# SiLU and merge gates computed by tanh, and the work of a recurrence pair shifted in time: a change to a fused encoder-block kernel

## The chip, the cores and the metric

The kernel runs on one core of a Trainium2 chip. The metric is the device time of one execution in microseconds (us). Five engines work beside each other, each through its own instructions in order: PE (TensorE, matmuls, with PEld for its weight loads), DVE (VectorE, elementwise), ACT (ScalarE, elementwise functions and casts), POOL (GpSimd, used here only to issue DMAs) and SP (SyncE, which issues the other DMAs). An engine that waits for a result of another holds up all that is queued behind it.

## The reference

One encoder block over 256 tokens of width 2048, all in float32:

```python
xn = rms_norm(x, norm_pre_w)
u_lru, g_lru, q, k, v, g_attn, m_lru, m_attn = split(xn @ w_in)
u = centred_depthwise_conv(u_lru, conv_w, conv_b)          # width 4
h = rg_lru(u, ..., reverse=False) + rg_lru(u, ..., reverse=True)
y_a = h * silu(g_lru)
y_b = windowed_gqa(partial_rope(q), partial_rope(k), v, sink) * silu(g_attn)
merged = sigmoid(m_lru) * (y_a @ w_proj_a) + sigmoid(m_attn) * (y_b @ w_proj_b)
x = x + rms_norm(merged @ w_out, norm_post_w)

def rg_lru(u, ...):                                        # 16 blocks of 128 channels
    r, i = sigmoid(block_matmul(u, w_r) + b_r), sigmoid(block_matmul(u, w_i) + b_i)
    log_a = -8 * r * softplus(-lam)
    return scan(a=exp(log_a), b=sqrt(-expm1(2 * log_a)) * i * u)
```

## The kernel before

**Products.** A float32 product is made of three passes on reduced parts: high part of the weights by high part of the activations, high by low, and low by high. The parts of activations are made by `lag_parts`/`parts_of` (a cast on ACT to the high part, a subtraction on DVE to the low part, line 123). Part of the products are saved by a seven-product scheme (`add_seven`, L634 on), whose operands are differences of quarters of x; four of those differences (`e1` to `e4`) are stored away in DRAM and taken back three times by `sums_back` (L889), which splits them again in `parts`.

**Steps and half steps.** The weights stream from DRAM as tiles of 128 x 2048 floats, 1 MB each. One tile is one *step* of the list `steps`, made of two half steps of about 2.3 us of PE work each. The program is written half step by half step: `at(hs, fn)` puts `fn` at a half step, `soon(fn, d)` puts it `d` half steps after the present one, and the work due at a half step is issued ahead of that half step's matmuls. So the order on every engine is fixed by these numbers. The names wh, wl, raw and chain with a number are the high and low part and the loaded tile of the step with that number. At the first half of step i, SP issues the load of tile i+3 (`fetch`), ACT casts tile i+2 to its high part (`ahead`, L991), and one half step later DVE takes the low part (`low`, L983). Some tiles are not loaded anew but made by adding a second tile in place to one that has been used: `low` then has POOL issue an accumulating DMA onto the same buffer (L989); such a tile is called chain. raw, wh and wl each have three buffers.

**The recurrence.** Eight calls of `lru_pair(n, b)`, for n = 0, 2, ... 14, take two blocks each, twelve half steps apart. Within a pair the list at L525 gives each piece its half step, counted from b (one more is added to those above 5): the convolution (`centre` on ACT with its centre tap, `conv` on DVE with three taps of two blocks), the parts of u, the gates' matmuls (`gates(0)`, `gates(1)`, two PSUM banks each, out of four that `bank` gives) and their sigmoids, then Tanh, Exp, Square, `scale1`, Sqrt, the product with the gated input, the scans and `gate_out`. ACT computes its functions from tables, and the compiler puts an ACT_TABLE_LOAD where the next function isn't in the one that stands: by its order one table serves Sigmoid and Tanh, one Exp and Tanh, and one Sqrt.

**SiLU and merge gates.** `silu_evac` (L537) takes the product of a gate path out of PSUM (`total`, L224: one copy on ACT, one addition on DVE), applies Sigmoid two half steps later and multiplies on DVE one after that. `gate_take` (L553) applies Sigmoid to the merge products; their gates multiply the projections in `take_pa` and `take_pb`, and `ms_part` (L848) copies the merged sum into the tile that the last product reads. The attention heads (`head`, L756) run from about 475 us on: scores, a maximum on DVE (L773), exponentials on ACT (L780), the normalisation (L786, L788), and a transposition of the probabilities p on PE (pt, L794).

Of the kernel before, what the change touches and what calls it, by code (L numbers as in the profile page):

```python
# [14 lines left out]
F32 = mybir.dt.float32  # L15
# [5 lines left out]
P = 128  # L21
# [62 lines left out]
def body(ctx, tc, x, xT, wall, wlru, pvec, npost, ident_d, mask_d, rope_d, out):  # L84
# [63 lines left out]
    def soon(fn, d=1):  # L148
        at(now[0] + d, fn)
# [216 lines left out]
    at(ROWS, row_scale)  # L366


    rtok = const.tile([P, 2], F32, name="rtok")

    def token_scale():
        for t in range(2):
            dg = small.tile([P, P], F32, tag="diag", name=f"diag{t}", bufs=1)
            nc.vector.tensor_tensor(dg, rbc[:, t * P:(t + 1) * P], ident, ALU.mult)
            nc.scalar.activation(dg, dg, AF.Copy, accum_out=rtok[:, t:t + 1])

    at(ROWS + 3, token_scale)

# [66 lines left out]
    def lru_pair(n, b):  # L445
# [71 lines left out]
        def gate_out():  # L517
            h = v["gr"]
            y = sgl[n // 4][:, n % 4:n % 4 + 2]
            nc.vector.tensor_tensor(h[:, 0:2], h[:, 0:2], h[:, 2:4], ALU.add)  # L520
            nc.vector.tensor_tensor(y, h[:, 0:2], y, ALU.mult)
            v.clear()

        at(max(b - 1, 7), load)
        for d, fn in (  # L525
            (-1, lambda: [centre(j) for j in range(2)]), (0, lambda: conv(0)), (1, lambda: conv(1)), (2, weights), (3, u_parts),
            (6, lambda: gates(0)), (7, lambda: gates(1)), (7, lambda: sigmoids(0)), (8, lambda: sigmoids(1)),
            (9, lambda: decays("th", AF.Tanh, cpos, 0)), (9, lambda: decays("th", AF.Tanh, cpos, 1)), (9, gated),
            (10, lambda: decays("a", AF.Exp, cneg, 0)), (11, lambda: decays("a", AF.Exp, cneg, 1)),
            (11, lambda: nc.scalar.activation(v["gr"], v["a"], AF.Square)), (12, scale1),  # L530
            (13, lambda: nc.scalar.activation(v["th"], v["th"], AF.Sqrt)),
            (16, lambda: nc.vector.tensor_tensor(v["gi"], v["gi"], v["th"], ALU.mult)),
            (17, scans), (19, gate_out),
        ):
            at(b + d + (G if d > 5 else 0), fn)

    def silu_evac(units_list, n, late=False):  # L537
        def done(ps):
            if n % 4 == 0:
                units_list.append(unit(f"sg{n}"))  # L540
            dst = units_list[n // 4][:, n % 4:n % 4 + 2]
            sg = unit(f"sig{n}", F32, (P, 2, S)) if late else half_unit(f"sig{n}", "p")
            total(dst, ps)
            soon(lambda: nc.scalar.activation(sg, dst, AF.Sigmoid), 2)
            soon(lambda: nc.vector.tensor_tensor(dst, dst, sg, ALU.mult), 3)
        return done

    def u_evac(n):
# [1 line left out]

    tm, sm, ms, whole = {}, {}, {}, {}

    def gate_take(units_of, c, t, ps, scale=1.0):  # L553
        if c not in units_of:
            units_of[c] = unit(f"mg{c}", F32, (P, 2, 512))
        nc.scalar.activation(units_of[c][:, t], ps, AF.Sigmoid, scale=scale)
        if units_of is sm and c < 2:
            return
        name = "sm" if units_of is sm else "tm"
        written[name, c] = written.get((name, c), 0) + 1  # L560
        if written[name, c] == 2:
            soon(lambda: gone.update({(name, c): put_away(f"{name}{c}", units_of.pop(c))}), AWAY)
# [1 line left out]
    gone, written = {}, {}  # L564

    def gate_evac(units_of, c, scaled=False):
        return lambda t, ps: gate_take(units_of, c, t, ps, rtok[:, t:t + 1] if scaled else 1.0)

    kv = {}

# [185 lines left out]
    def head(hd, qh, ql, b):  # L756
# [49 lines left out]

        def gate_out():
            y = sga[g][:, j]
            nc.vector.tensor_tensor(y, v["o"][:, 0], y, ALU.mult)
            v.clear()  # L810

        for d, fn in ((0, scores), (1, expo), (2, powers), (3, normalise), (5, flip), (6, p_parts), (9, values), (10, gate_out)):
# [12 lines left out]

    def take_pa(c, t, d):
        g = tm[c][:, t]
        nc.vector.tensor_tensor(g, d, g, ALU.mult)

    def take_pb(c, t, d):  # L830
        g = sm[c][:, t]
        nc.vector.tensor_tensor(g, d, g, ALU.mult)
        nc.vector.tensor_tensor(g, tm[c][:, t], g, ALU.add)
        if t == 1:
            held = {}
            soon(lambda: ms_flip(c, held), 3)
            for q in range(2):
                soon(lambda q=q: ms_part(c, q, held), 4 + q)
# [9 lines left out]
    def ms_part(c, q, held):  # L848
        a = pair_unit(f"ms{2 * c + q}")
        ms[2 * c + q] = a  # L850
        if q == 0:
            whole[c] = unit(f"mw{c}")
        w = whole[c][:, 2 * q:2 * q + 2]
        nc.scalar.copy(w, held.pop(q))
        lag_parts(a[:, :, 0], a[:, :, 1], w)

    def branch(name, m, y, take):
# [31 lines left out]
    def sums_back(r):  # L889
        def back(d, n):  # L890
            l = take_back(f"e{r}{d}", kept[d], F32R, (P, 8, P))

            def parts():
                h = unit(f"e{r}{d}h", F32R, (P, 8, P))
                lag_parts(h, l, l.bitcast(F32))
                again[r][d] = (h, l)

            at(n - 7, parts)

        for d, n in (("e1", 4), ("e4", 6), ("e3", 8), ("e2", 10)):  # L900
            n = 2 * steps.index(woven[14 * (r + 1) + n])
            at(n - 16, lambda d=d, n=n: back(d, n))
# [192 lines left out]
```

## Time and profile before

| | |
|---|---|
| runs shown | 887.29, 888.70, 888.81 us; median 888.7 |
| profiled execution | 889.92 us, its span 888.1 us |
| granted TensorE clock, mean | 0.997 |
| busy: PE, PEld | 871.8 us, 746.2 us |
| busy: DVE, ACT, POOL | 717.8 us, 648.5 us, 44.1 us |
| DMA | 230.89 MB, mean 260 GB/s |

The span is the time from the first to the last instruction in the trace; the time of the execution has some more around it. Busy times are sums over the instructions of an engine, and PE's matmuls are pipelined, so that a busy PE says only that it had a matmul under way. A row of the trace's timeline gives start and duration in us, engine, line of the kernel, operation, output<-input with shapes and types, the count, and in brackets the idle time ahead of it with the releaser: the engine and line whose result came last. The row of a group of instructions gives the line, engine, operation, operands and count, then busy us in all and the mean in ns, then the idle time ahead of it. In a row of the waits the three numbers are the total in us, how many times, and the longest.

### The profile page before, as it was taken

The page shows a single profiled execution, that of the slowest core. Times are in us where ns is not written, and L with a number is a line of the kernel's source. Part 1 is how long each engine was busy: PE and PEld are TensorE (multiplying, and loading weights), DVE is VectorE, ACT ScalarE, POOL GpSimd, SP SyncE. Part 2 cuts the span into 40 slices and gives each one's busy share as a digit, 9 for nine tenths or more (in the row PEclk, how much of TensorE's full clock was granted, in tenths as well). Part 3 has the DMA queues.
Part 4 walks back from the last instruction along what each step waited for, and adds up shares of the span by engine and source line. Part 5 has one row for each costly group of instructions (what it writes and reads, how often), then busy time and mean ns, then how long its engine had stood idle before and what let it go on. Part 6 is the DMA issues. An engine that isn't in the chain of part 4 may idle for free.

```text
span 888.1 us, 11537 instructions
## 1 busy us (share of the span) xinstructions
PE 871.8 (98%) x4494; PEld 746.2 (84%) x4494; DVE 717.8 (81%) x763; ACT 648.5 (73%) x762; POOL 44.1 (5%) x57
## 2 busy tenths in 40 slices
PE   8999999999999999999999999999999999999996
PEld 8888888888888888888877788888888888888885
DVE  5987897978969699897967878778897767757886
ACT  6978579787796977879688877967966454547653
POOL 0000000010000100000000000000000000100000
PEclk9999999999999999999999999999999999999998
DMA  8746977997998988888877976897966996998894
GB/s 323 273 169 243 324 212 265 279 308 204 315 339 301 238 229 291 234 341 245 248 208 280 245 270 214 203 278 275 260 249 237 271 246 194 320 287 317 227 275 161
DMA packets 38935, 230.89 MB, mean 260 GB/s; under 512 B 4320, under 2 KB 5216, under 8 KB 15456
## 3 DMA queue, kind: packets, MB, share of 16 engines
q1 hardware_dynamic: 31248, 179.19, 53.6%
q0 software_dynamic: 7200, 50.33, 29.4%
q8 instruction: 35, 0.57, 0.2%
q10 hardware_dynamic: 432, 0.63, 0.2%
q14 instruction: 20, 0.16, 0.0%
HBM read 220.70 MB, written 9.44 MB: 259 GB/s over the span
## 4 chain that ended last, share of the span: by engine, by line
PE 77%; ACT 9%; DVE 6%; DMA 5%; issue 2%; DVEq 0%; SPq 0%; ACTq 0%
PE ga L209 5%; PE gl L209 5%; ACT wh L995 3%; PE u L209 3%; DVE wl L985 3%; DMA chain<-wall_dram 3%; PE gl L211 3%; PE ga L211 3%; PE pa__5505 L240 2%; PE q__4370 L240 2%; PE q__4968 L240 2%; PE ml__622 L240 2%; PE ml L240 2%; PE pa__5865 L240 2%; PE o__6883 L240 2%; PE o L240 2%
## 5 line engine op out<-in xcount | busy, mean ns | idle before, releaser
L985 DVE TENSOR_TENSOR wl<-raw,wh 128x2048 fp32r<-128x2048 f32 x112 | 256.0, 2288 | 60.3 <-ACT wh L995 60.3
L995 ACT CAST wh<-raw 128x2048 fp32r<-128x2048 f32 x112 | 214.0, 1912 | 56.5 <-DMA raw<-wall_dram 20.8
L985 DVE TENSOR_TENSOR wl<-chain,wh 128x2048 fp32r<-128x2048 f32 x68 | 155.4, 2287 | 37.9 <-ACT wh L995 37.9
L995 ACT CAST wh<-chain 128x2048 fp32r<-128x2048 f32 x68 | 129.9, 1912 | 59.6 <-DMA chain<-wall_dram 23.5
L989 POOL DMA_DIRECT2D chain<-wall_dram x46 | 40.2, 874 | 768.6 <-DVE wl L985 761.0
L209 PE MATMUL ga<-xn,wh 128*128 128x512 f32 x256 | 62.9, 391 | 0.0
L209 PE MATMUL gl<-xn,wh 128*128 128x512 f32 x256 | 62.2, 390 | 0.0
L209 PEld LDWEIGHTS gl<-xn,wh 128*128 128x128 f32 x256 | 47.6, 188 | 9.3
L209 PEld LDWEIGHTS ga<-xn,wh 128*128 128x128 f32 x256 | 47.4, 188 | 9.1
L209 PE MATMUL u<-xn,wh 128*128 128x512 f32 x192 | 46.8, 391 | 0.0
L209 PEld LDWEIGHTS u<-xn,wh 128*128 128x128 f32 x192 | 35.6, 188 | 7.1 <-ACT wh L995 0.3
L211 PEld LDWEIGHTS ga<-xn,wl 128*128 128x128 f32 x256 | 32.8, 191 | 1.3
L211 PEld LDWEIGHTS gl<-xn,wl 128*128 128x128 f32 x256 | 32.8, 191 | 1.2
L211 PE MATMUL gl<-xn,wl 128*128 128x256 f32 x256 | 33.2, 283 | 0.0
L211 PE MATMUL ga<-xn,wl 128*128 128x256 f32 x256 | 33.2, 283 | 0.0
L211 PEld LDWEIGHTS u<-xn,wl 128*128 128x128 f32 x192 | 24.6, 191 | 0.9
L211 PE MATMUL u<-xn,wl 128*128 128x256 f32 x192 | 24.9, 283 | 0.0
L470 DVE SCALAR_TENSOR_TENSOR up<-up,pv 128x255 f32<-128x255 f32 (+1 forms) x48 | 22.8, 482 | 1.1
L122 ACT CAST ph<-pt 128x512 fp32r<-128x512 f32 x16 | 9.4, 585 | 17.2 <-PE pt L794 13.2
L509 DVE SCALAR_TENSOR_TENSOR th<-gr,th 128x1024 f32<-128x1024 f32 x8 | 9.8, 1225 | 13.6 <-ACT gr L530 13.6
L399 PE MATMUL u_ps<-xs,wh 128*128 128x256 f32 x128 | 18.6, 288 | 1.8 <-ACT wh L115 1.8
L190 PE MATMUL gate<-uh,lwh 128*128 128x256 f32 x64 | 18.2, 285 | 2.1 <-ACT gi L494 2.1
(568 smaller groups left out, 1978.8 us busy)
## 6 DMA issues: line engine op xcount, KB each, us to landing
raw<-wall_dram SPq DMA_DIRECT2D x115, 1024.0 KB, 7.0
chain<-wall_dram POOLq DMA_DIRECT2D x46, 1024.0 KB, 9.6
chain<-wall_dram SPq DMA_DIRECT2D x22, 1024.0 KB, 4.9
lraw<-wlru_dram SPq DMA_DIRECT2D x8, 512.0 KB, 7.1
raw<-wall_dram SPq DMA_DIRECT2D x4, 512.0 KB, 8.0
tm_away<-mg SPq DMA_DIRECT2D x4, 512.0 KB, 9.4
xee_away<-xee SPq DMA_DIRECT2D x4, 512.0 KB, 8.3
ya_away<-sg SPq DMA_DIRECT2D x4, 512.0 KB, 10.3
```

What stands on the lines that cost most here:

```text
L122: nc.scalar.copy(h, src)
L190: nc.tensor.matmul(ps, wh, xh, start=start, stop=False)
L209: nc.tensor.matmul(ps, wh[:, sl], a, start=k == 0, stop=k == KT - 1)
L211: nc.tensor.matmul(ps[:, 1], wl[:, sl], a[:, 0], start=False, stop=False)
L240: nc.tensor.matmul(got[t], a[:, m], w[:, j * 512:(j + 1) * 512], start=k == 0 and m == 0 and not low, stop=low and k == KT - 1)
L399: nc.tensor.matmul(ups[b // 2][:, b % 2, 0], w[:, sl], a[:, m], start=k == 0 and n == 0, stop=k == KT - 1 and n == 2)
L470: nc.vector.scalar_tensor_tensor(u[:, a:b], up[:, a + tap - 2:b + tap - 2], cw[:, tap:tap + 1], u[:, a:b], ALU.mult, ALU.add)
L509: nc.vector.scalar_tensor_tensor(v["th"], v["gr"], 1.0, v["th"], ALU.add, ALU.mult)
L985: nc.vector.tensor_tensor(lows[i][:, sl], t, highs[i][:, sl].bitcast(F32), ALU.subtract)
L989: nc.gpsimd.dma_start(raws[n], wall[rows_of[steps[n][0]]], accum_op=ALU.add)
L995: nc.scalar.copy(highs[i][:, sl], t)
```

## The change

In place of sigmoid(z) stands (1 + tanh(z/2)) / 2. SiLU's Sigmoid and the merge gates' become Tanh with a scale of 0.5; the addition of 1 goes into the following DVE multiplication, which becomes a SCALAR_TENSOR_TENSOR; and the factor one half goes into the recurrence's and the heads' `gate_out` and into the copy of `ms_part`. The recurrence's own gates stay Sigmoid. In a pair, the convolution is put twelve half steps ahead (the centre tap nineteen), the second gates and all from the second sigmoids to Sqrt one half step later, and behind Sqrt comes a one-column activation `warm` that brings the next Sigmoid table (Tanh for the last pair). The splits of x's differences in `sums_back` are put three half steps sooner.

```diff
         for t in range(2):
...
-            nc.scalar.activation(dg, dg, AF.Copy, accum_out=rtok[:, t:t + 1])
+            nc.scalar.activation(dg, dg, AF.Copy, scale=0.5, accum_out=rhalf[:, t:t + 1])
...
-            nc.vector.tensor_tensor(y, h[:, 0:2], y, ALU.mult)
+            nc.vector.scalar_tensor_tensor(y, h[:, 0:2], 0.5, y, ALU.mult, ALU.mult)
...
-            (-1, lambda: [centre(j) for j in range(2)]), (0, lambda: conv(0)), (1, lambda: conv(1)), (2, weights), (3, u_parts),
-            (6, lambda: gates(0)), (7, lambda: gates(1)), (7, lambda: sigmoids(0)), (8, lambda: sigmoids(1)),
-            (9, lambda: decays("th", AF.Tanh, cpos, 0)), (9, lambda: decays("th", AF.Tanh, cpos, 1)), (9, gated),
-            (10, lambda: decays("a", AF.Exp, cneg, 0)), (11, lambda: decays("a", AF.Exp, cneg, 1)),
-            (11, lambda: nc.scalar.activation(v["gr"], v["a"], AF.Square)), (12, scale1),
-            (13, lambda: nc.scalar.activation(v["th"], v["th"], AF.Sqrt)),
+            ((-20, lambda: [centre(j) for j in range(2)]) if n else (-1, lambda: [centre(j) for j in range(2)])), (-12 if n else 0, lambda: conv(0)), (-11 if n else 1, lambda: conv(1)), (2, weights), (3, u_parts),
+            (6, lambda: gates(0)), (7, lambda: sigmoids(0)), (8, lambda: gates(1)), (9, lambda: sigmoids(1)),
+            (10, lambda: decays("th", AF.Tanh, cpos, 0)), (10, lambda: decays("th", AF.Tanh, cpos, 1)), (10, gated),
+            (11, lambda: decays("a", AF.Exp, cneg, 0)), (12, lambda: decays("a", AF.Exp, cneg, 1)),
+            (12, lambda: nc.scalar.activation(v["gr"], v["a"], AF.Square)), (13, scale1),
+            (14, lambda: nc.scalar.activation(v["th"], v["th"], AF.Sqrt)),
+            (14, lambda: nc.scalar.activation(warm, eps, AF.Sigmoid if n < 14 else AF.Tanh)),
             (16, lambda: nc.vector.tensor_tensor(v["gi"], v["gi"], v["th"], ALU.mult)),
             (17, scans), (19, gate_out),
...
-            soon(lambda: nc.scalar.activation(sg, dst, AF.Sigmoid), 2)
-            soon(lambda: nc.vector.tensor_tensor(dst, dst, sg, ALU.mult), 3)
+            soon(lambda: nc.scalar.activation(sg, dst, AF.Tanh, scale=0.5), 2)
+            soon(lambda: nc.vector.scalar_tensor_tensor(dst, sg, 1.0, dst, ALU.add, ALU.mult), 3)
...
-        nc.scalar.activation(units_of[c][:, t], ps, AF.Sigmoid, scale=scale)
+        nc.scalar.activation(units_of[c][:, t], ps, AF.Tanh, scale=scale)
...
-            nc.vector.tensor_tensor(y, v["o"][:, 0], y, ALU.mult)
+            nc.vector.scalar_tensor_tensor(y, v["o"][:, 0], 0.5, y, ALU.mult, ALU.mult)
...
-        nc.vector.tensor_tensor(g, d, g, ALU.mult)
+        nc.vector.scalar_tensor_tensor(g, g, 1.0, d, ALU.add, ALU.mult)
...
-        nc.scalar.copy(w, held.pop(q))
+        nc.scalar.activation(w, held.pop(q), AF.Copy, scale=0.5)
...
-            at(n - 7, parts)
+            at(n - 10, parts)
```

The built programs have 41 table loads before and 29 now on ACT, and eight one-column activations more. PE, SP and POOL have as many instructions as before, SP and POOL in the same order.

The first place is PE at the gates of pair 14, near 450 us. A name such as gate14_11 is the PSUM bank of the pair's gates (second block, second direction), mbn7_ is the accumulator of a seven-product step, and wh95 its weights. Before:

```order
L650 MATMUL mbn7_3818<-wl94_3866,e1e2h_3829 128x512 x4
L190 MATMUL gate14_10_3970<-uh14_3880,lwh14_3861 128x256
...
L192 MATMUL gate14_11_3977<-uh14_3880,lwl14_3862 128x256
L650 MATMUL mbn7_3818<-wh95_3901,e1e2h_3829 128x512
L650 MATMUL mbn7_3818<-wh95_3901,e1e2_3700 128x512
...
L604 MATMUL q0p_4003<-ident_97,q0t_3932 128x128 x8
```

And of the change:

```order
L651 MATMUL mbn7_3836<-wl94_3873,e1e2h_3799 128x512 x4
L651 MATMUL mbn7_3836<-wh95_3908,e1e2h_3799 128x512
L651 MATMUL mbn7_3836<-wh95_3908,e1e2_3716 128x512
...
L190 MATMUL gate14_10_3992<-uh14_3887,lwh14_3868 128x256
...
L192 MATMUL gate14_11_3999<-uh14_3887,lwl14_3869 128x256
L605 MATMUL q0p_4006<-ident_97,q0t_3939 128x128 x8
```

The matmuls of step 95's first half now stand ahead of the pair's second gates.

The second place is ACT behind the gates of the same pair, from about 460 to 477 us. th14, a14 and gr14 are the pair's decays and gates, q0p a rotated query, mg3 a merge gate, wh98 to wh101 the casts of the weights. Before:

```order
L505 ACT_TABLE_LOAD
...
L556 ACT_TABLE_LOAD
...
L505 ACT_TABLE_LOAD
L505 ACTIVATE a14_4048<-gr14_3984,cneg_163 128x256 x2
L530 ACTIVATE gr14_3984<-a14_4048 128x1024
L995 CAST wh99_4075<-chain87_3603 128x2048
L531 ACT_TABLE_LOAD
L531 ACTIVATE th14_4019<-th14_4019 128x1024
L995 CAST wh100_4107<-raw100_4069 128x2048
L995 CAST wh101_4133<-raw101_4104 128x2048
```

And of the change:

```order
L557 ACTIVATE mg3_4057<-mbt0_3311 128x512
L505 ACT_TABLE_LOAD
L505 ACTIVATE a14_4075<-gr14_3977,cneg_163 128x256 x2
L996 CAST wh99_4079<-chain87_3607 128x2048
L505 ACTIVATE a14_4075<-gr14_3977,cneg_163 128x256 x2
L530 ACTIVATE gr14_3977<-a14_4075 128x1024
L996 CAST wh100_4113<-raw100_4073 128x2048
L531 ACT_TABLE_LOAD
L531 ACTIVATE th14_4048<-th14_4048 128x1024
L532 ACT_TABLE_LOAD
L532 ACTIVATE warm_77<-eps_78 128x1
L996 CAST wh101_4141<-raw101_4110 128x2048
```

Sqrt with its table load stood ahead of wh100's cast and now stands behind it, followed by a further table load and `warm`. The three table loads for the first Exp of the decays (L505), for the merge gates (L556) and for the second Exp are one load now: the merge gates, as a Tanh at L557, stand ahead of it and need none.

The third place is ACT in pair 6, near 255 us, where the copy of `total` (the SiLU's product out of PSUM) is followed by the weight casts. Before:

```order
L226 COPY total_2330<-ga6_2243 128x512
L995 CAST wh52_2332<-raw52_2282 128x2048
L122 CAST e0e1h_2341<-e0e1_2148 128x1024
L544 ACT_TABLE_LOAD
L544 ACTIVATE sig6_2329<-sg4_1877 128x512
L995 CAST wh53_2353<-raw53_2324 128x2048
```

And of the change:

```order
L226 COPY total_2343<-ga6_2241 128x512
L996 CAST wh52_2345<-raw52_2284 128x2048
L531 ACT_TABLE_LOAD
L531 ACTIVATE th6_2254<-th6_2254 128x1024
L532 ACT_TABLE_LOAD
L532 ACTIVATE warm_77<-eps_78 128x1
L545 ACTIVATE sig6_2342<-sg4_1886 128x512
L996 CAST wh53_2365<-raw53_2337 128x2048
```

Sqrt, ahead of `total` before, now stands behind it, with two table loads where there was one. On DVE of the same pair, before:

```order
L521 TENSOR_TENSOR sg4_1702<-gr6_2201,sg4_1702 128x512
L985 TENSOR_TENSOR wl55_2419<-chain47_2055,wh55_2418 128x2048
L227 TENSOR_TENSOR up10_2458<-u10_2380,total_2459 128x512
L985 TENSOR_TENSOR wl56_2462<-raw56_2414,wh56_2461 128x2048
L470 SCALAR_TENSOR_TENSOR up8_2006<-up8_2006,pv_95 128x254
L470 SCALAR_TENSOR_TENSOR up8_2006<-up8_2006,pv_95 128x255 x2
L123 TENSOR_TENSOR e0e4_2327<-e0e4_2327,e0e4h_2475 128x1024
```

And of the change:

```order
L521 SCALAR_TENSOR_TENSOR sg4_1706<-gr6_2192,sg4_1706 128x512
L123 TENSOR_TENSOR e0e4_2340<-e0e4_2340,e0e4h_2430 128x1024
L986 TENSOR_TENSOR wl55_2433<-chain47_2058,wh55_2432 128x2048
L227 TENSOR_TENSOR up10_2473<-u10_2392,total_2474 128x512
L986 TENSOR_TENSOR wl56_2477<-raw56_2426,wh56_2476 128x2048
```

The low part of the stored difference e0e4 now stands ahead of the low part of step 55's weights, and the convolution of the next pair (L470) no longer stands behind them.

More of the change, by code (lines that the diff above doesn't have):

```diff
@@ L366, in body @@
     at(ROWS, row_scale)
-    rtok = const.tile([P, 2], F32, name="rtok")
+    rhalf = const.tile([P, 2], F32, name="rhalf")
     def token_scale():
@@ L551, in body, with gate_take @@
     tm, sm, ms, whole = {}, {}, {}, {}
-    def gate_take(units_of, c, t, ps, scale=1.0):
+    def gate_take(units_of, c, t, ps, scale=0.5):
         if c not in units_of:
             units_of[c] = unit(f"mg{c}", F32, (P, 2, 512))
-        nc.scalar.activation(units_of[c][:, t], ps, AF.Sigmoid, scale=scale)
+        nc.scalar.activation(units_of[c][:, t], ps, AF.Tanh, scale=scale)
         if units_of is sm and c < 2:
@@ L566, in gate_evac @@
     def gate_evac(units_of, c, scaled=False):
-        return lambda t, ps: gate_take(units_of, c, t, ps, rtok[:, t:t + 1] if scaled else 1.0)
+        return lambda t, ps: gate_take(units_of, c, t, ps, rhalf[:, t:t + 1] if scaled else 0.5)
     kv = {}
@@ L827, in take_pa @@
         g = tm[c][:, t]
-        nc.vector.tensor_tensor(g, d, g, ALU.mult)
+        nc.vector.scalar_tensor_tensor(g, g, 1.0, d, ALU.add, ALU.mult)
     def take_pb(c, t, d):
         g = sm[c][:, t]
-        nc.vector.tensor_tensor(g, d, g, ALU.mult)
+        nc.vector.scalar_tensor_tensor(g, g, 1.0, d, ALU.add, ALU.mult)
         nc.vector.tensor_tensor(g, tm[c][:, t], g, ALU.add)
```

## The prediction

> **What bounds the kernel now.** First the engine totals, then the stretches of 50 us, then what the weight loads of TensorE waited for, since PE runs its instructions in order and each such wait stops it.
>
> ```profile
> span 888.1 us, 11537 instructions
> PE 871.8 (98%) x4494; PEld 746.2 (84%) x4494; DVE 717.8 (81%) x763; ACT 648.5 (73%) x762; POOL 44.1 (5%) x57
> ```
> ```profile
> 400.00:450.00 50.00, 50.00 (x242) 42.24 (x242) 39.36 (x36) 37.39 (x39) 4.38 (x5) 1.00 0.90 254
> 450.00:500.00 50.00, 45.06 (x222) 36.95 (x222) 40.47 (x55) 45.72 (x63) 2.60 (x3) 1.00 0.78 222
> ```
> ```profile
> PEld pt L794 <- ACT p L788: 3.5, 4, 1.7
> PEld gate L190 <- ACT gi L494: 2.5, 2, 2.0
> PEld mlq L650 <- DVE wl L985: 1.1, 1, 1.1
> PEld q__4035 L240 <- ACT wh L995: 1.0, 1, 1.0
> PEld gate L191 <- DVE ul L123: 0.3, 1, 0.3
> PEld u L209 <- ACT wh L995: 0.3, 1, 0.3
> ```
>
> PE is busy 98% of the span, and the change keeps every matmul, so only PE's stops can be won. The columns of the stretches are length, then busy time (and instructions) of PE, PEld, DVE, ACT and POOL, the granted clock and DMA. Between 450 and 500 us PE loses 5 us and ACT is the fullest engine, 45.7 of 50; in the stretch before, nothing is lost. The six rows of waits (total, times, longest) are PE's stops after the start: 3.5+2.5+1.1+1.0+0.3+0.3 = 8.7 us. That is the ceiling. No table load, cast or convolution counts unless one of these stops hangs on it, or a new one arises.
>
> **What costs the same.** Tanh takes the place of Sigmoid on the same shapes, and a SCALAR_TENSOR_TENSOR that of a TENSOR_TENSOR:
>
> ```profile
> L509 DVE SCALAR_TENSOR_TENSOR th<-gr,th 128x1024 f32<-128x1024 f32 x8 | 9.8, 1225 | 13.6 <-ACT gr L530 13.6
> L532 DVE TENSOR_TENSOR gi<-gi,th 128x1024 f32<-128x1024 f32 x8 | 9.7, 1217 | 0.0
> L545 DVE TENSOR_TENSOR sg<-sg,sig 128x512 f32<-128x512 f32 x16 | 10.9, 684 | 0.0
> L556 ACT ACT_TABLE_LOAD x6 | 7.7, 1283 | 0.1
> L780 ACT ACT_TABLE_LOAD x6 | 7.7, 1283 | 0.1
> ```
>
> 1225 against 1217 ns on the same shape: the 56 exchanged VectorE instructions cost nothing (bounds: below, nothing can be won on them; above, the rule under the rivals). The half-scaled copies of ms_part stay one pass over 512 columns. Twelve table loads fall away (41 to 29): those of L556 and L780 that alternated while heads ran, 12 x 1.283 = 15.4 us of ACT. Most of it lies beside PE's work, so I count it only at the stops. Per pair of the recurrence the three loads stay (Exp, Sqrt, and one moved from the SiLU to right behind Sqrt), plus a one-column activation that I take at 0.3 us from the 128x2 row below (bounds 0 and 0.5, the shortest 128x256 ACTIVATE).
>
> **The stop at 453 us (second gates one half step behind).**
>
> ```profile
> 447.74 1.90 ACT L995 CAST wh<-chain 128x2048 fp32r<-128x2048 f32 x1 [7.74 <-DMA chain<-wall_dram]
> 449.55 1.07 ACT L578 COPY q0t<-q__3753 128x512 f32<-128x512 f32 x2
> 450.50 1.91 ACT L995 CAST wh<-raw 128x2048 fp32r<-128x2048 f32 x1
> 452.67 0.48 ACT L494 ACTIVATE gi<-gate,pv 128x256 f32<-128x256 f32 x1
> ```
> ```profile
> 433.28 0.86 POOL L989 DMA_DIRECT2D chain<-wall_dram  x1 [2.66 <-DVE wl L985]
> ```
> ```profile
> 453.21 0.19 PEld L190 LDWEIGHTS gate<-uh,lwh 128*128 128x128 f32 x1 [2.01 <-ACT gi L494]
> 454.03 0.19 PEld L650 LDWEIGHTS mbn<-wh,e1e 128*128 128x128 f32 x1
> 454.26 0.19 PEld L650 LDWEIGHTS mbn<-wh,e1e2h 128*128 128x128 f32 x1
> ```
>
> Pair 14's fourth gate bank is only free when ACT has read the first, and ACT is late because it stood 7.74 us before a cast (step 95) whose chained weights landed at 447.7. In the new order six matmuls of mbn7 (0.23 us each by the last two rows, 1.4 us) go ahead of the second gates. The release itself, 453.2, stays tied to the landing. That transfer is issued at 433.3, when wl91 is done. By the additions below wl91 comes at most 1.7 us later (a cast 1.0, a difference's split of 512 columns 0.7), but the queue still holds the transfer of the step ahead, whose wl comes earlier in the pair; I take 0.5 us for the landing (bounds 0 and 1.7; nearer to 0, as 14.4 us pass from issue to landing, most of it behind others). So PE leaves the gates having gained **1.4 - 0.5 = 0.9 us** over the old run (bounds -0.3 and 1.4 plus what is won before). This covers everything ahead of it: the 0.5 us stop of pair 10 (same cause, landing not involved) and the 0.3 of ul10 and of u go away, but PE only arrives sooner at the same landing.
>
> **What the moved work does to the weights of each pair.** In each pair the Sqrt, its table load, the next table load and the one-column activation now stand between `total` and the weight cast, and lag parts of x's differences are split three half steps sooner.
>
> ```profile
> 219.50 2.28 DVE L985 TENSOR_TENSOR wl<-chain,wh 128x2048 fp32r<-128x2048 f32 x1
> 271.28 2.28 DVE L985 TENSOR_TENSOR wl<-chain,wh 128x2048 fp32r<-128x2048 f32 x1
> 277.71 1.22 DVE L123 TENSOR_TENSOR e0e<-e0e,e0e4h 128x1024 fp32r<-128x1024 f32 x1
> 224.50 2.95 DVE L470 SCALAR_TENSOR_TENSOR up<-up,pv 128x254 f32<-128x254 f32 x6
> ```
> ```profile
> 222.39 0.87 PEld L650 LDWEIGHTS mlq<-wl,xn 128*128 128x128 f32 x4
> 275.03 0.87 PEld L650 LDWEIGHTS kvq<-wl,e0e1h 128*128 128x128 f32 x4
> 203.16 0.57 ACT L226 COPY total<-ga 128x512 f32<-128x512 f32 x1
> 205.55 1.28 ACT L544 ACT_TABLE_LOAD   x1
> ```
>
> Low parts of pair 4 end at 221.78, loaded at 222.39: 0.6 us in hand; pair 6 has 275.03 - 273.56 = 1.5. Sqrt and its load take 1.28 + 1.06 = 2.34 us (the rows of 205.55 here and of 472.60 below). ACT may start `total` that much sooner, but hardly more than 1.7 us, as PE's result must be there; it pays 2.34 + 0.3 after it: the cast, and VectorE's row behind it, come 1.0 us later. Pair 4: 0.35 us of new wait. Pair 6: 1.0 + 1.22 (e0e4's low parts now ahead of wl55) - 1.5 = 0.7. Pairs 10 and 12 I put below pair 4, at 0.1 and 0.2. Pair 2 (mlq's 1.1 us in the list of waits) 0.2 more; pair 8, without a difference there, none. Sum 1.55 us; bounds 0 (ACT idle enough) and 1.9 each, a whole cast. They fall before the landing, where PE waits anyway: PE would arrive at the last gate with some 0.4 us left to wait, so they cost nothing up to there, and one for one beyond 2.0 us. The convolution's 2.95 us and the two centres per pair move twelve and twenty half steps ahead into VectorE's and ACT's idle time (the releaser is ACT's casts there), at nothing; if that cover were gone they would add to the same weights, at most 2.95 a pair. What was taken away behind `u` only widens margins. SP's and POOL's queues keep their order; only the moment of a chained issue moves with wl.
>
> **The stops at 475, 486 and 496 us.**
>
> ```profile
> 469.39 1.89 ACT L995 CAST wh<-chain 128x2048 fp32r<-128x2048 f32 x1
> 472.60 1.06 ACT L531 ACTIVATE th<-th 128x1024 f32<-128x1024 f32 x1
> 473.56 3.69 ACT L995 CAST wh<-raw 128x2048 fp32r<-128x2048 f32 x2
> 480.96 0.28 ACT L781 ACTIVATE es<-nm,pv 128x2 f32<-128x2 f32 x1
> 485.42 0.91 ACT L788 ACTIVATE p<-p,rd 128x256 f32<-128x256 f32 x2 [2.38 <-DVE rd L786]
> ```
> ```profile
> 482.05 0.69 DVE L514 TENSOR_TENSOR_SCAN gr<-a,gi 128x256 f32<-128x256 f32 x1
> 485.16 0.17 DVE L786 RECIPROCAL rd<-dn 128x2 f32<-128x2 f32 x1
> ```
> ```profile
> 485.98 0.14 PEld L794 LDWEIGHTS pt<-ident,p 128*128 128x128 f32 x1 [1.68 <-ACT p L788]
> 496.36 0.14 PEld L794 LDWEIGHTS pt<-ident,p 128*128 128x128 f32 x1 [1.33 <-ACT p L788]
> ```
>
> I walk ACT's queue from 453.2 + 0.5. At 475 PE waited for wh100, cast from 473.56. Ahead of it now two loads are gone (2.6 us) and Sqrt with its load (2.34 us) stands behind it: about 4.9 less 0.5, so ready near 471; PE comes at 473.5. That stop goes: **1.0 us**. Then come load, Sqrt, load, one column (3.9 us) and wh101, which ends at 477.1 as before. VectorE then runs wl101 (2.3) and what it ran from 482.05 to 485.33, four scans, a difference and the reciprocal (3.3): 482.7. PE's row came 0.65 us behind the reciprocal's end, so 483.35; PE, 0.9 + 1.0 us sooner, is there at 484.30 - 1.9 = 482.4 and still waits some 1.0, where it waited 1.68: **0.6 us**. From there p1: between p0's scaling at 485.42 and PE's row at 496.36 lie 10.9 us, of them two loads (L556, L780) that fall away, 2.6. Set off at 482.8 that gives 491.1 to 492, as q1t and a cast may wait for their inputs; PE comes at 495.03 - 2.5 = 492.5. That stop goes: **1.6 us**, its 1.33 and some 0.25 in which the array drains (taken from the start-to-start gaps of PE's rows there). Later heads have no stop now, and less ACT work.
>
> Sum: 0.9 + 1.0 + 0.6 + 1.6 = **4.1 us**. The profiled execution is the span of 888.1 and some 1.8 us around it, 889.9; less 4.1 that is 885.8. The runs shown have a median of 888.7, which I put the change on: **884.6 us**.
>
> **Rivals.** (a) *Everything goes*: all stops but mlq's vanish and no pair waits; 8.7 - 1.1 = 7.6, less the 0.2 us that the array still drains in each: 882. For it: the landing may come sooner, as wl93 is done sooner. Against: VectorE's order at 483.
> (b) *The chained transfer becomes the bound*: step 95's weights, in flight from 433.3 to 447.7 beside two ordinary weight tiles, fall behind them by one tile's 4.1 us (1 MB at the 254 GB/s of the stretch from 400 to 450); the walk shifts whole, 4.1 - 4.1 = 0: 888.7. For it: wl91 comes later; against: the queue's earlier transfer hardly moves.
> (c) *Slower*: the weight casts of pairs 2, 4, 6, 10 and 12 slip by a further whole cast (1.9 us) each, since Sqrt's operand, VectorE's scale1, is itself late in the compressed chain. Price 5 x 1.9 = 9.5, the first 1.0 free: 893. It turns the sign once the pairs' waits grow by 5.1 us. Against: ACT's square ends before `total` may start in each pair that I walked.
> (d) *The exchanged instruction is slow*: at 1.37 us instead of 0.68 for silu's product and the recurrence's gate, 1.4 us more ahead of those same five weights, 7 - 1.0 = 6: 890.6. The two rows of 1225 and 1217 ns speak against it. The Trainium skill, "Vector Engine (DVE) Microarchitecture Reference", "7. Points that are easy to get wrong", states such a halved rate for this instruction with two non-bf16 SBUF sources; by that rule this rival holds, and this trace disagrees.
> (e) *It doesn't do what it says*, the loads staying: excluded, as the built order has 29.
>
> **How the numbers follow.** Forecast 0.66, (a) 0.07, (b) 0.14, (c) 0.10, (d) 0.03. The range takes the forecast with its bounds (landing, 0.9 to 1.2 either way; the pairs' waits up to 2 us more) and reaches into (a) and (b): 881.7 to 887.9. About 0.2%, 1.8 us, can be told from no change: faster 0.74, same 0.15, slower 0.11.
>
> **What would show it.** Right: the gi and q rows gone from PEld's waits or below 0.6 us, one pt stop near 1.3 left, VectorE's wl in PEld's waits at two or more places near 222 and 275, 29 table loads, ACT below 635 us. Wrong: wl waits above 3 us in all (c), a wait of wh for the chain behind which PE stands (b), or SCALAR_TENSOR_TENSOR of 512 columns far above 0.69 us (d).

## The result, and the profile after

| | before | changed |
|---|---|---|
| median of 13 runs | 889.53 us | 884.29 us |
| lowest and highest | 887.29, 890.81 | 882.98, 888.74 |
| profiled execution: span | 888.1 us | 883.2 us |

The ratio is 0.9949, with a 95% interval of 0.9937 to 0.9962: 0.5% faster, 3.4 to 5.6 us. First the totals of the engines:

```profile
span 883.2 us, 11533 instructions
PE 871.4 (99%) x4494; PEld 746.1 (84%) x4494; DVE 718.1 (81%) x763; ACT 635.8 (72%) x758; POOL 44.2 (5%) x57
```

PE has the work of before, 4.9 us of span are gone, and ACT is busy 12.7 us less. The stretches from 400 us on, in the columns of the prediction (length, busy PE, PEld, DVE, ACT, POOL, clock, DMA):

```profile
400.00:450.00 50.00, 50.00 (x246) 42.37 (x245) 41.06 (x36) 38.82 (x41) 4.37 (x5) 1.00 0.92 259
450.00:500.00 50.00, 50.00 (x254) 42.47 (x253) 43.21 (x61) 45.13 (x67) 2.60 (x3) 1.00 0.88 262
```

Between 450 and 500 us PE now loses nothing, where it lost 5 us, though ACT is nearly as full as it was (45.1 against 45.7). What the weight loads waited for (total, times, longest), without the first 15 us:

```profile
PEld mlq L651 <- DVE wl L986: 2.4, 3, 0.9
...
PEld mbp L651 <- DVE wl L986: 0.9, 1, 0.9
PEld kvq L651 <- DVE wl L986: 0.6, 1, 0.6
...
PEld gate L190 <- ACT gi L494: 0.2, 1, 0.2
```

The stops on ACT are gone (p, wh, and the second gates but for 0.2 us); waits for low parts of weights have grown from 1.1 to 3.9 us. Two groups and the rows of ACT at the last pair:

```profile
L546 DVE SCALAR_TENSOR_TENSOR sg<-sig,sg 128x512 f32<-128x512 f32 x16 | 11.0, 687 | 4.9 <-ACT sig L545 4.9
L532 ACT ACT_TABLE_LOAD x8 | 10.3, 1283 | 0.1
```
```profile
446.46 1.91 ACT L996 CAST wh<-chain 128x2048 fp32r<-128x2048 f32 x1 [4.79 <-DMA chain<-wall_dram]
...
472.79 0.20 ACT L532 ACTIVATE warm<-eps 128x1 f32<-128x1 f32 x1
472.90 1.90 ACT L996 CAST wh<-raw 128x2048 fp32r<-128x2048 f32 x1
...
480.42 0.91 ACT L789 ACTIVATE p<-p,rd 128x256 f32<-128x256 f32 x2 [2.63 <-DVE rd L787]
```

The cast of step 95, which waits for the chained weights, starts at 446.46 where it started at 447.74. That is the row that the forecast had the other way round, and the experiments turn on it.

### The profile page after: what moved, and what is told of

It is laid out like the page before. It is cut to its first block, busy times and chain, and to the rows that moved or that the text cites. A ratio compares the mean times of both kernels' runs of the same rounds, so it can differ in the third digit from the quotient of the medians.

```text
span 883.2 us, 11533 instructions
## 1 busy us (share of the span) xinstructions
PE 871.4 (99%) x4494; PEld 746.1 (84%) x4494; DVE 718.1 (81%) x763; ACT 635.8 (72%) x758; POOL 44.2 (5%) x57
## 4 chain that ended last, share of the span: by engine, by line
PE 83%; DMA 5%; ACT 5%; DVE 5%; issue 1%; DVEq 0%; SPq 0%; ACTq 0%
PE gl L209 6%; PE ga L209 4%; PE gl L211 3%; DVE wl L986 3%; DMA chain<-wall_dram 3%; PE pa__5513 L240 2%; PE q__4378 L240 2%; PE u L209 2%; PE q__4976 L240 2%; PE q__4035 L240 2%; PE ml__622 L240 2%; PE ml L240 2%; PE pa__5873 L240 2%; PE o__6891 L240 2%; PE o L240 2%; PE pb__6665 L240 2%
## 5 line engine op out<-in xcount | busy, mean ns | idle before, releaser
L470 DVE SCALAR_TENSOR_TENSOR up<-up,pv 128x255 f32<-128x255 f32 (+1 forms) x48 | 22.7, 481 | 1.1
L116 DVE TENSOR_TENSOR wl<-raw,wh 128x1024 fp32r<-128x1024 f32 (+1 forms) x14 | 15.0, 1070 | 6.3 <-ACT wh L115 6.2
L774 DVE CUSTOM_DVE_ANT_0 p<-sc,mask,pv 128x256 f32<-128x256 f32 x32 | 14.2, 480 | 5.8 <-PE sc L192 5.8
```

The lines of the kernel that those rows point to most:

```text
L116: nc.vector.tensor_tensor(l, src, h.bitcast(F32), ALU.subtract)
L470: nc.vector.scalar_tensor_tensor(u[:, a:b], up[:, a + tap - 2:b + tap - 2], cw[:, tap:tap + 1], u[:, a:b], ALU.mult, ALU.add)
L774: nc.vector.tensor_tensor_reduce(p[:, t], sc[:, t], mask[:, t], P ** -0.5, sk, ALU.add, ALU.max, m[:, t:t + 1])
```

## The experiments

Each kernel was timed against the kernel before in five rounds on the same chip; ratios are to that kernel. Below, a stop is an extra time between the starts of two neighbouring matmuls, beyond the usual one for their shape.

### The two halves of the change

The first kernel keeps the tanh form and has the order of before:

```diff
-            ((-20, lambda: [centre(j) for j in range(2)]) if n else ...
+            (-1, lambda: [centre(j) for j in range(2)]), (0, lambda: conv(0)), ...    # the list of before
-            at(n - 10, parts)
+            at(n - 7, parts)
```

> The tanh form of the SiLU and merge gates alone; the order of the work in a pair and the splits of x's differences as before. Theory 1 (the gain is the table loads at the last pair and the heads; the new order in the earlier pairs only costs): the gates' stop at 453 stays at about 2.0 us, the stops at 475, 486 and 496 (0.9, 1.7, 1.6) go, and no new waits for wl: 889.5 - 4.2 = 885.3 us. Theory 2 (the new order carries the gain): only the stop at 496, which has a table load of its own on either side, goes: 889.5 - 1.6 = 887.9 us, with stops left at 453, 475 and 486.

Measured: 891.2 us, ratio 1.0026 (1.0010 to 1.0043), slightly slower than before. The waits, and ACT at pair 14's gates:

```profile
PEld gate L190 <- ACT gi L494: 4.4, 3, 2.6
```
```profile
450.50 1.92 ACT L995 CAST wh<-raw 128x2048 fp32r<-128x2048 f32 x1
452.44 1.28 ACT L493 ACT_TABLE_LOAD   x1
453.74 0.47 ACT L493 ACTIVATE gr<-gate,pv 128x256 f32<-128x256 f32 x1
```

The stops at 475, 486 and 496 are gone, as Theory 1 said, but the gates of pairs 8, 12 and 14 now stop PE (0.9, 0.9 and 2.6 us). Without a Sigmoid in the SiLU, the table with Sigmoid in it isn't loaded until the next pair's gates ask for it, right where PE waits for their banks: SiLU's Tanh joins the Exps in one run on their table. (The Trainium skill, "ScalarE activation tables: per-element evaluation and per-set limits", "Table sets in the compiler and the runtime", says that the loads are placed by the greedy longest run; the row at 452.44 agrees.) Both theories fell.

How the 891.2 us come about isn't shown, though. The execution in the trace took 886.99 us, the lowest of the twelve, and its span of 885.2 us is below that of the kernel before, in spite of these stops. What the other executions have on top is in no trace; the granted clock gives a hint, which is taken up at `tanh_warm` below.

The second kernel has the new order and the earlier splits, with Sigmoid kept:

```diff
-            soon(lambda: nc.scalar.activation(sg, dst, AF.Tanh, scale=0.5), 2)
+            soon(lambda: nc.scalar.activation(sg, dst, AF.Sigmoid), 2)
...
-            (14, lambda: nc.scalar.activation(warm, eps, AF.Sigmoid if n < 14 else AF.Tanh)),
+            (14, lambda: nc.scalar.activation(warm, eps, AF.Sigmoid)),
```

> The new order of the pairs, the one-column activation behind Sqrt (Sigmoid for all pairs) and the earlier splits, with Sigmoid kept. Theory 1: the 453 stop goes, with a net of 0.5 us against the weights' waits of 1.3 us that the earlier pairs add; the 475 stop goes (0.9); those at 486 and 496 stay in good part, since the merge gates' loads are still there: 889.5 - 2 = 887.5 us. Theory 2: nearly the whole gain is here: 885 to 886 us.

Measured: 884.57 us, ratio 0.9959 (0.9943 to 0.9975), the changed kernel's time within the error. Its waits behind the start, and four of its table loads from ACT's rows:

```profile
PEld mlq L651 <- DVE wl L986: 1.9, 3, 0.9
...
PEld kvq L651 <- DVE wl L986: 0.7, 1, 0.7
...
PEld mbp L651 <- DVE wl L986: 0.2, 1, 0.2
```
```profile
459.23 1.28 ACT L505 ACT_TABLE_LOAD   x1
...
472.65 1.28 ACT L781 ACT_TABLE_LOAD   x1
...
479.18 1.28 ACT L557 ACT_TABLE_LOAD   x1
...
483.41 1.28 ACT L781 ACT_TABLE_LOAD   x1
```

No stop is left at 453, 475, 486 or 496, although the loads at 479 and 483 still lie between p0 and p1. And the three loads near 461 to 466 have become one here as well: with the Exps half a step later, the merge gates' Sigmoid finds the table that Tanh of the decays used. Theory 2 stands, and the time is 0.4 us below the range that it gave.

### Which part of the order

The changed kernel, with the splits of x's differences back:

```diff
-            at(n - 10, parts)
+            at(n - 7, parts)
```

> The changed kernel with the splits of x's stored differences back at seven half steps ahead. Theory 1 (the wait for the low parts of steps 55 and 79 comes from the split that now stands ahead of them): the waits of kvq (0.6) and mbp (0.9) go, PE is there 1.1 us sooner at pair 14's gates, where the first read of a bank leaves it about 1.2 us of room: 884.3 - 1.0 = 883.3 us, gate wait still below 0.3. Rival (the landing of step 95's chained weights sets the place at 453 whatever comes ahead): a gate wait of about 1 us comes back and the time stays at 884.3 us.

Measured: 886.9 us, ratio 0.9982 (0.9968 to 0.9995), slower than the changed kernel's 0.9949, where one reading had 1 us less and the other no change. A gates' stop of 1.3 us is back at 454.5, and step 95's cast starts at 449.04 instead of 446.46. The changed kernel with the convolution back:

```diff
-            ((-20, lambda: [centre(j) for j in range(2)]) if n else (-1, ...)), (-12 if n else 0, lambda: conv(0)), (-11 if n else 1, lambda: conv(1)), ...
+            (-1, lambda: [centre(j) for j in range(2)]), (0, lambda: conv(0)), (1, lambda: conv(1)), ...
```

> The changed kernel with the convolution (centre tap and three taps) back at its place ahead of u's parts. Theory 1 (the convolution was hidden before and is hidden after): within 0.5 us of the changed kernel, 884.3 us, with the same waits for wl. Rival (the convolution stood ahead of weights that have little in hand now): new waits for wl of up to 2.95 us in a pair behind u, summing to 2 to 4 us: 886 to 888 us.

Measured: 884.22 us, ratio 0.9947 (0.9930 to 0.9965). The convolution was hidden before and is hidden now.

So the earlier splits, which the prediction had priced as a cost, were a candidate for the gain. Alone in the kernel before (only n - 7 to n - 10):

> The kernel before with nothing changed but the splits of x's differences, ten instead of seven half steps ahead. Theory 3 (in pair 14 the split e1e2 stands between the low parts of steps 90 and 91, so the two accumulating transfers are issued 4.7 us apart instead of 3.5, the ordinary load that follows overlaps the second one less, and its weights land about 10.7 us after their issue instead of 13 to 14.5; ACT is early from there on): landing 2 to 3 us sooner than before, the gates' stop at 453 below 0.7 us (2.1 before), the stops at 475, 486 and 496 smaller by as much as ACT is ahead, against 0.5 to 1 us of new waits at steps 55 and 79: 885.5 us. Rival (the split only costs, as the prediction had it): stops at 453 to 496 unchanged, 889 us.

Measured: 885.84 us, ratio 0.9967 (0.9954 to 0.9979). Its waits:

```profile
PEld pt L794 <- ACT p L788: 3.5, 4, 1.7
...
PEld gate L190 <- ACT gi L494: 0.9, 1, 0.9
PEld mlq L650 <- DVE wl L985: 0.8, 1, 0.8
```

The stops at 453 and 475 are gone (the gates' stop left stands at 187 us); those at 486 and 496 stay whole, 1.70 and 1.58, against what Theory 3 said of ACT's lead. The new waits at steps 55 and 79 did not come.

The second gates alone, in the kernel before:

```diff
-            (6, lambda: gates(0)), (7, lambda: gates(1)), (7, lambda: sigmoids(0)), (8, lambda: sigmoids(1)),
+            (6, lambda: gates(0)), (7, lambda: sigmoids(0)), (8, lambda: gates(1)), (9, lambda: sigmoids(1)),
```

> The kernel before with only the second gates and their sigmoids one half step later, tanh, exp and Sqrt where they were. Theory 3: PE isn't stopped at 453 (at most 0.7 us), but the landing at 447.7 and with it ACT's lag stay, so that PE, some 1.4 us sooner, waits more at 475, 486 and 496 instead: 888 us. Rival (the place of the second gates carries the gain): stop at 453 gone and the later ones no longer than before: 886.5 us or less.

Measured: 887.13 us, ratio 0.9983 (0.9972 to 0.9993).

```profile
PEld pt L794 <- ACT p L788: 3.6, 4, 1.7
...
PEld q__4035 L240 <- ACT wh L995: 1.1, 1, 1.1
...
PEld mbq L650 <- ACT wh L995: 0.8, 1, 0.8
PEld mbq L650 <- DVE wl L985: 0.6, 1, 0.6
```

At 453 only 0.3 us is lost, but PE, 2.2 us ahead there (0.7 us of it from the first 60 us of this execution), meets ACT's lag in new waits at 471 and 473 and leaves 475 only 0.8 us ahead, as Theory 3 said. The time lies between the two theories. The reverse, the second gates back in the changed kernel (the diff above, turned round):

> The changed kernel with the second gates and second sigmoids back at the half steps of before, all else as changed. Theory 3 (the landing was what mattered): landing at about 446.4 as in the changed kernel, a gates' stop of 0.3 to 1.2 us at 453 and a share of the 0.5 us stop of pair 10 come back, no stop at 475 to 496: 885.2 us. Rival (the place of the second gates carries the gain): gates' stops of 2 us and more, 886.5 us.

Measured: 885.78 us, ratio 0.9962 (0.9949 to 0.9976); its interval and the changed kernel's overlap.

```profile
PEld gate L190 <- ACT gi L494: 1.8, 1, 1.8
```

This stop stands at 348, in pair 10, where a share of 0.5 us was expected, and none at 453: with the landing early, pair 14's second gates needn't be moved.

### The load of the Sigmoid table

The tanh form alone with the one-column activation behind Sqrt, where Sqrt stood before:

```diff
             (13, lambda: nc.scalar.activation(v["th"], v["th"], AF.Sqrt)),
+            (13, lambda: nc.scalar.activation(warm, eps, AF.Sigmoid if n < 14 else AF.Tanh)),
```

> The tanh form alone, as in tanh_alone, and a one-column activation behind Sqrt that brings the Sigmoid table back (Tanh for pair 14). Theory 3 (with tanh alone the load of the Sigmoid table, 1.3 us, lands right ahead of the first gates' sigmoids, where PE waits for their banks): the gates' stops of pairs 8 and 12 (0.9 each) go, that of pair 14 falls from 2.7 to about 2: 891.2 - 2.5 = 888.7 us. Rival (the exchanged instructions are slow somewhere, or the landing alone makes tanh_alone slow): 890.5 to 891.5 us.

Measured: 893.72 us, ratio 1.0059 (1.0043 to 1.0075), slower still. The waits, and ACT at pair 6:

```profile
PEld gate L190 <- ACT gi L494: 5.2, 3, 3.9
PEld u L209 <- ACT wh L996: 4.1, 3, 1.9
```
```profile
259.01 1.28 ACT L532 ACT_TABLE_LOAD   x1
260.30 0.20 ACT L532 ACTIVATE warm<-eps 128x1 f32<-128x1 f32 x1
260.41 0.57 ACT L226 COPY total<-ga 128x512 f32<-128x512 f32 x1
260.88 1.91 ACT L996 CAST wh<-raw 128x2048 fp32r<-128x2048 f32 x1
```

The stops of pairs 8 and 12 did go, but the load and the activation now stand ahead of `total` and the weights' cast, and PE waits 4.1 us for casts at three of the u steps. Pair 4 has a gates' stop of 1.1 us, and that of pair 14 grew to 3.9, behind a landing 18.4 us after the issue. The changed kernel, which puts the load behind Sqrt and behind the cast, has none of these stops; what share the load has there in the waits for low parts of pairs 4, 6 and 10, no run separates.

This execution lost time in one more way. The page has the granted TensorE clock in tenths of full speed, over 40 equal slices of the span:

```profile
PEclk9999999999999999999989999999999999999999
```

In the slice with the 8 the clock is 0.50 from 462 to 466 us and 1.00 again from 468 on. PE, stopped for 3.9 us up to 461.6, then ran at half clock and fell back by another 2.8 us. In the other traces, whose stops behind the start are 2.6 us at most, no stop is followed by such a stretch. This execution's mean clock is 0.994. Four of the six executions of `tanh_warm` and seven of the twelve of `tanh_alone` have a mean of 0.995 or less, while the 27 of the kernel before that were timed with `tanh_alone` have 0.997 or more. So a stretch at half clock is likely a part of `tanh_alone`'s time too; no trace of such an execution of it shows that.

### The landing of step 95's weights

Only one split stands near the accumulating transfers, that of e1e2 in pair 14. It alone, in the kernel before, ahead of the low part of step 91 (so that the two transfers are issued 4.7 us apart), and then, with a 9 for the 10, between the low parts of steps 91 and 92 (so that they stay 3.5 apart and only the next ordinary load is later):

```diff
-            at(n - 7, parts)
+            at(n - (10 if (r, d) == (1, "e2") else 7), parts)
```

> The kernel before with a single split moved, that of e1e2 (pair 14), which then stands between the low parts of steps 90 and 91. Theory 3 (this one split makes the whole effect of split_alone, through the landing of step 95's weights): landing about 15 us after the first of the two accumulating transfers is issued (18.0 in the kernel before, 14.9 in split_alone), no stop at 453 and 475, those at 486 and 496 as before: 885.5 us. Rival (the gain of split_alone is spread over several pairs): 887.5 us or more, a stop at 453 of over 1 us.

> As one_split, but the split of e1e2 stands behind the low part of step 91 and ahead of that of step 92: the two accumulating transfers are again 3.5 us apart, and only the ordinary load that follows step 92 is issued 1.2 us later. Theory 3a (the ordinary load's start against the two transfers decides, not their distance): landing 15 to 15.5 us after the first issue, time as one_split, 885.5 us. Theory 3b (the distance of the two issues decides): landing 17 us or more after the first issue, stop at 453 back, 888 us.

Measured: 886.76 us, ratio 0.9977 (0.9966 to 0.9987), and 887.58 us, ratio 0.9991 (0.9976 to 1.0006). In both the stop at 453 is gone and that at 475 below 0.3 us. The rows of before and of the changed kernel that the landing hangs on (POOL's issues, and SP's next ordinary load):

```profile
429.76 0.86 POOL L989 DMA_DIRECT2D chain<-wall_dram  x1 [13.38 <-DVE wl L985]
...
435.11 0.33 SPq L176 DMA_DIRECT2D raw<-wall_dram  x1
```
```profile
431.24 0.86 POOL L990 DMA_DIRECT2D chain<-wall_dram  x1 [14.41 <-DVE wl L986]
435.90 0.86 POOL L990 DMA_DIRECT2D chain<-wall_dram  x1 [3.80 <-DVE wl L986]
...
437.73 0.33 SPq L176 DMA_DIRECT2D raw<-wall_dram  x1
```

The same times from the trace of every kernel; the cast is that of step 95, and the last column the time from the first issue to it:

```
kernel               issue 1  issue 2  ordinary   cast  cast - issue 1
before                429.76   433.28   435.11   447.74   18.0
second_gates_alone    429.34   432.87   434.70   446.92   17.6
split_back            431.69   435.22   437.04   449.04   17.4
tanh_alone            431.06   434.59   436.41   447.74   16.7
tanh_warm             437.75   441.28   443.10   456.15   18.4
one_split_behind      430.22   433.75   436.71   445.43   15.2
one_split             429.13   433.79   435.62   444.44   15.3
split_alone           427.52   432.19   434.01   442.46   14.9
after_one_split       431.82   436.48   438.31   447.03   15.2
last_pair_and_split   431.50   436.17   437.99   446.74   15.2
order_alone           429.00   433.66   435.48   444.41   15.4
conv_back             430.35   435.01   436.84   445.71   15.4
gates_together        431.89   436.56   438.38   447.33   15.4
after                 431.24   435.90   437.73   446.46   15.2
```

In the first five the ordinary load is issued 5.4 us after the first transfer, in the others 6.5 us; in one_split_behind with the issues 3.5 us apart. Theory 3a holds for the landing, 3b doesn't. How the packets share, counted from the trace in packets that ended (accumulating queue q0, ordinary queue q1):

```
us          before q0, q1     after q0, q1
434 - 436      51     0         50     0
436 - 438      58     0         51     0
438 - 440      35    14         62     0
440 - 442      29    28         52     1
442 - 444      38    35         35    33
444 - 446      25    83         33    69
446 - 448       7   104          1   118
```

Alone, the accumulating transfers move 25 to 31 packets a us; beside an ordinary load about 17. In the changed kernel they are alone until 442, before only until 438. That one_split_behind's time is not clearly below the kernel before, with the stops of 453 and 475 gone in its profile, stays open: its runs spread over 885.6 to 891.5 us. Its trace gives one hint: PE loses 1.6 us at 328 and 341, in pair 10, where `one_split`, with the same order up to there, loses nothing. That is a difference between executions, not between the edits.

### Less of the change

The changed kernel with only e1e2's split early:

> The changed kernel with all splits back at seven half steps but that of e1e2. Theory 3 (the other splits moved only cost, by the waits for low parts at steps 55 and 79): landing as in the changed kernel, the waits of kvq and mbp (0.4 and 0.7 us) go in part: 884.3 - 0.7 = 883.6 us. Rival (the other splits' place helps elsewhere, or the pairs' waits come back under other names, as in split_back): 884.3 us or more.

Measured: 885.93 us, ratio 0.9977 (0.9962 to 0.9992): the rival.

```profile
PEld mbn L651 <- DVE wl L986: 1.3, 1, 1.3
PEld kvn L651 <- DVE wl L986: 1.2, 2, 0.9
...
PEld kvq L651 <- DVE wl L986: 0.9, 1, 0.9
```

The first two waits, at 329 and 436, are new. On VectorE the splits of e0e2 and e1e3 stand here, each waiting 2.5 us for ACT's cast with the gated product, the SiLU's product and a weight's low part behind it:

```profile
315.23 1.23 DVE L123 TENSOR_TENSOR e0e<-e0e,e0e2h 128x1024 fp32r<-128x1024 f32 x1 [2.53 <-ACT e0e2h L122]
...
421.71 1.23 DVE L123 TENSOR_TENSOR e1e<-e1e,e1e3h 128x1024 fp32r<-128x1024 f32 x1 [2.52 <-ACT e1e3h L122]
```

In the changed kernel these two splits are done some 10 us sooner. So the early place saves here and costs in pair 10, whose wait of 0.9 us (mbp) is gone in this kernel. The wait of pair 6 (kvq) is still there, 0.9 us against 0.6 in the changed kernel, so it doesn't come from the split.

Last, the kernel before with the new list for pair 14 alone (convolution in place, no one-column activation), e1e2's split early, Sigmoid everywhere:

```diff
-        for d, fn in (
-            (-1, lambda: [centre(j) for j in range(2)]), (0, lambda: conv(0)), (1, lambda: conv(1)), (2, weights), (3, u_parts),
+        for d, fn in (new if n == 14 else old) + (
...
-            at(n - 7, parts)
+            at(n - (10 if (r, d) == (1, "e2") else 7), parts)
```

> The kernel before with Sigmoid everywhere, the split of e1e2 moved and the new order of the pieces (no one-column activation, convolution in its place) in pair 14 alone. Theory 3 (the changed order is worth something only at pair 14, and costs in the others): no stops at 453 to 496, and no waits for wl in the pairs but that at 170 (1.0) and a gates' stop of 0.5 at 345: 888.7 - 6.2 = 882.5 us, better than the changed kernel. Rival (the order is wanted in every pair): 884.5 us or more.

Measured: 883.68 us, ratio 0.9940 (0.9923 to 0.9957).

```profile
PEld gate L191 <- DVE ul L123: 1.4, 1, 1.4
PEld mlq L660 <- DVE wl L995: 1.2, 2, 0.9
...
PEld gate L190 <- ACT gi L494: 0.6, 1, 0.6
```

No stop from 453 on. Its interval holds the changed kernel's ratio, so it is as fast, not shown to be faster; and it does without tanh, without the moved convolution and without a new order in the seven pairs ahead. It differs from `one_split` by the list of pair 14 alone, and takes 883.68 us against 886.76. `one_split` still has the stops at 486 and 496 whole (1.7 and 1.6 us) and this kernel doesn't, so that list is worth about 3 us there. Which of its pieces does it, the Exps on one table load or Sqrt behind the cast, no run separates. The time lies between the two that were expected.

## Why the prediction was right, and where its steps were wrong

The time came out at 884.29 us for 884.6 forecast, and the four stops gave 4.9 us of span for 4.1. That the time lies so near is luck in part: the gain was larger than forecast (5.2 us between the medians, for 4.1), and the 13 runs of the kernel before have a median 0.8 us above the 888.7 that the forecast was put on. By the starts of the same matmuls in both traces:

| term | forecast | measured |
|---|---|---|
| up to the rotation behind pair 14's gates (453) | 0.9 | 0.6 |
| wh100 (475) | 1.0 | 0.9 |
| p0 (486) | 0.6 | 1.8 |
| p1 (496) | 1.6 | 1.6 |

**What bounds it** was right: nothing but PE's stops counted. 12.7 us of ACT's work fell away, and `order_alone`, which keeps the merge gates' loads, is as fast. Tanh alone makes the kernel slower. Two signs of being right failed in their size: no pt stop is left, where one near 1.3 us was expected, and ACT is busy 635.8 us, where less than 635 was.

**The landing** was the step that failed: "I take 0.5 us for the landing", later, bounds 0 and 1.7. The second transfer was issued 2.6 us later, beyond the 1.7 that the forecast took as the most, and its weights were there 1.28 us sooner. The step counted the move of VectorE's instruction against POOL's issue, but not against SP's: the split that delays wl91 delays wl92 too, hence the ordinary load that takes the bandwidth. The prediction's "only the moment of a chained issue moves" leaves out exactly that load.

**The pairs' waits** were near in their sum and mis-sized in each place: 1.55 us forecast, and by 383 us PE was 1.4 us behind the kernel before. Pair 4 took 1.4 us of stops where 0.35 was forecast; pair 6 0.4 (0.7), pair 10 0.7 (0.1), pair 12 none (0.2); pair 2 lost 0.4 less, and the gates' stop of 0.5 in pair 10 is gone. In pair 6 the forecast put 1.22 us down to the split, and `after_one_split` keeps the wait without it. Nor were these waits hidden at the gates, as forecast. ACT's second read of the first bank, a row of 0.48 us, starts at 451.40 and so ends near 451.9, while PE came to the second gates at 453.14, so PE had 1.2 us of room there, and by that 1.2 us of what the pairs lost is lost in the time as well. The stop of 2.1 us is gone whole, and less the 1.5 us by which PE came later it gives the 0.6 of the first row. The forecast's 0.9 was 1.4 less 0.5, from other steps, so it is luck that it lies near.

**p0** followed: ACT's walk was to set out 0.5 us late and set out 1.3 us early, so wh101 ended at 474.8 and not at 477.1 (0.5 us of that isn't traced), and PE found p0 ready at 482.8 instead of waiting 1.0 us. **p1** came out as forecast, but its reason is only one of two: in `tanh_alone` the missing loads clear it, in `order_alone` it clears with both loads in place. The split alone clears neither.

**The second gates** were credited with the stop at 453. They do clear it (`second_gates_alone`), but then PE meets ACT's lag in later waits and 1.5 us is left; with the landing early the same stop is gone without them.

**What costs the same** held. The exchanged VectorE instruction took 687 ns for 684. The Trainium skill, "Vector Engine (DVE) Microarchitecture Reference", "7. Points that are easy to get wrong", states half the rate for this instruction with two SBUF sources that aren't bf16; this kernel's traces disagree, and the rival that rested on it fell. Of the other rivals, the slower one, weight casts that slip behind Sqrt's chain, showed its sign without its price: the waits for wl are 3.9 us, above the 3 us in all that the prediction named as a sign of being wrong, and the kernel is still faster. Something like it appeared in `tanh_warm`, where one table load and one activation ahead of the cast go with waits of 4.1 us at three steps.

## What to carry to other kernels

A wait on a transfer depends on what else is on the DMA queues, so when an instruction moves, follow every load that its engine's order releases, on all queues, and not only the one whose wait is in question. Removing work from an engine that isn't the bound was worth nothing by itself here; look first which later instruction inherits the table, the slot or the lag. And split a change of many parts before crediting any of them: here one of its parts (tanh) costs alone, one (the convolution) does nothing, and a split that looked like a cost carried most of the gain.

## What the runs showed of the hardware that was not expected

Accumulating transfers on the software queue moved 25 to 31 packets a us alone and about 17 with an ordinary load beside them. With the ordinary load issued 1.1 us later, the second of two such transfers was there some 2 to 3 us sooner behind the first issue: 17.4 and 18.0 us against 15.2 and 15.3, in the two pairs of kernels that differ by that split alone, and 15.2 in `one_split_behind`, where the two transfers stay as far apart as before.

Behind a stop of 3.9 us TensorE's granted clock was 0.50 for some us (`tanh_warm`), which cost 2.8 us on top of the stop; behind the stops of up to 2.6 us in the other traces it was 1.00. One trace shows this, once.

And executions of one program differ by some us: `tanh_alone`, profiled at a span of 885.2 us and 886.99 us in all, had a median of 891.2 us over 12 runs, 886.99 being the lowest of them. The traces of `second_gates_alone`, `tanh_warm` and `last_pair_and_split` are of the slowest of their runs, that of `order_alone` of the fastest. Where the difference arises isn't shown in general; after their first 60 us the profiled executions already lie up to 2.2 us apart. A single profile of such a kernel is not its time.
